# Keeping the split, transposed input of layer 0 in DRAM between two projections, and taking the gate projection two heads at a time

## The chip, the core and the metric

The kernel runs on one core of a Trainium2 chip. The metric is the device time of one execution in microseconds (us); the time before is the median of three runs. Compute engines of the core: TensorE (PE, matmuls; its weight loads are shown as PEld), VectorE (DVE), ScalarE (ACT) and GpSimd (POOL). SyncE (SP) issues all of this kernel's DMAs from one queue that works in order: a DMA that has to wait holds the ones behind it.

## The reference, cut to what matters

Two layers over x of 2048 rows by 1024. The first is sparse latent attention, the second a gated delta rule; each ends with a gated per-layer embedding. The change lies in the input projection of the first layer:

```
h = rms_norm(x, norm_w[0])
proj = h @ w_in
c_q, c_kv, k_idx, w_idx, z = jnp.split(proj, [256, 512, 640, 648], axis=-1)
c_q = rms_norm(c_q, g_cq); c_kv = rms_norm(c_kv, g_kv); k_idx = rms_norm(k_idx)
score = einsum("bqhs,bqh->bqs", relu(einsum("bqhd,bsd->bqhs", q_idx, k_idx)), w_idx)
_, sel = lax.top_k(score, 256)            # causal, per query
... attention over the selected latents gives o ...
return (o * jax.nn.silu(z)) @ w_out       # z has 8 heads of 128
```

So the same normalised h is needed by the latents (c_q, c_kv, k_idx, w_idx) and by the gates z.

## The kernel before, in words

A product of two float32 matrices is made of three matmuls: each operand is split into a high part (ACT copies it to the matmul's type) and a low part (the rest; DVE subtracts when the source is in PSUM, POOL when it is in SBUF). `split`, `split_sb` and `mm3_step` (lines 71 to 92) do this.

Phase 1 (up to about 865 us of the profiled execution) has two scopes. In `latents` the rows go in four super blocks (sb) of 512. `enter(sb, 3)` loads four blocks of 128 rows of x (`load_x`), normalises them, transposes each on PE against `ident` (8 transposes of 128x128, L209, tile `xT`), and splits the result from PSUM into `hT` (L78 on ACT, L79 on DVE). `latents(sb)` then multiplies hT with the weights of c_q, k_idx, c_kv and w_idx, while `enter` of the next super block is woven between. The normalised x is also stored to DRAM (`xn_d`, L189).

In `scores` four kinds of streams are woven on all engines: `index` (matmuls `il`, ACT relu `rl`, DVE adds into `score`), `topk` (13 rounds of counting above a threshold, half of the blocks on DVE, L729, half on ACT, L727, with some small POOL instructions that set the next threshold; then a selection on DVE that ends in `pen`, which SP stores and ACT sums, `penj`, L805), and the stream `rest`: `gates_z` for the four super blocks, then `proj_k` and `proj_v1`, then `proj_q`. `PLAN`, `WORK` and the weights of the parts give every piece of a stream a place on one scale, `weave` takes the pieces in the order of these places, and a scheduler then sets the order on each engine. At run time each engine works in that order.

`gates_z(sb)` needs hT again. Before the change it loads the normalised x back from `xn_d` (L179), transposes it again (32 transposes a super block, woven as `enter(sb, 2)`) and splits it again into four tiles of tag `c8`; then, head by head, it takes two weight tiles (`win`: a load `wr`, a split on ACT, L86, and POOL, L87, into a tile `w` of 4 buffers; the raw tiles `raw` have 3) and makes 24 matmuls of 512 columns (`pz`). ACT applies SiLU to the head (L370) and SP stores it (L371). After the fourth super block `proj_k` loads four tiles of the latents c_kv into the same four `c8` buffers.

## Time and profile before

| | before |
|---|---|
| median of 3 runs | 3472.86 us (3471.24 to 3486.31) |
| profiled execution | 3468.28 us, span 3466.6 us, mean granted clock 0.981 |
| PE busy | 3321.1 us (96% of the span) |
| DVE, ACT, POOL busy | 2102.7, 1882.7, 943.2 us |
| mean DMA rate | 90 GB/s |

PE is busy nearly all the time, and it works in order, so time is won where PE has less to do or waits less. The profiled execution is 4.6 us under the median of the runs. The profile counts overlapping matmuls once; a single matmul's duration is longer than the distance to the next.

### The profile page before, as it was taken

How to read it: one execution, taken by the hardware profiler on the slowest of the kernel's cores; microseconds unless marked ns; L12 is line 12 of the kernel's file. 1: busy time of each engine (PE TensorE's matmuls, PEld its weight loads, DVE VectorE, ACT ScalarE, POOL GpSimd, SP SyncE). 2: the span in 40 equal slices, each digit the busy share in tenths (PEclk: the TensorE clock that was granted, in tenths of full speed). 3: DMA queues.
4: the chain of work that ended last, by engine and by line, in shares of the span. 5: the costliest groups of instructions: out<-in, count | busy, mean ns of one | idle time of the engine just before them, and what ended most of it. 6: DMA issues, size and time to landing. Idle time of an engine off the chain costs nothing.

```text
span 3466.6 us, 52296 instructions
## 1 busy us (share of the span) xinstructions
PE 3321.1 (96%) x19082; PEld 2786.5 (80%) x19082; DVE 2102.7 (61%) x4566; ACT 1882.7 (54%) x3319; POOL 943.2 (27%) x1620
## 2 busy tenths in 40 slices
PE   8999988988899999999999999999999999899999
PEld 6778777877799999888887788887788888778887
DVE  5367896865588888622225667667667676633222
ACT  5366947675677777543335565555555555433221
POOL 2022435145645444211100221222121222321100
PEclk9999998999899999999999999999999999899999
DMA  6322344442522222422223222213222222233211
GB/s 218 114 77 68 102 148 145 172 152 98 183 78 85 80 85 74 136 95 64 72 64 94 58 50 55 53 45 93 54 58 50 58 51 57 86 130 116 73 34 72
DMA packets 325294, 311.71 MB, mean 90 GB/s; under 512 B 69448, under 2 KB 272808, under 8 KB 322984
## 3 DMA queue, kind: packets, MB, share of 16 engines
q1 hardware_dynamic: 325032, 308.33, 29.8%
q8 instruction: 150, 2.46, 0.3%
q14 instruction: 112, 0.92, 0.1%
HBM read 212.85 MB, written 95.42 MB: 89 GB/s over the span
## 4 chain that ended last, share of the span: by engine, by line
PE 53%; DVE 11%; DMA 4%; ACT 2%; POOL 2%; issue 2%; SPq 0%; DVEq 0%; ACTq 0%; POOLq 0%
PE pgm L91 3%; PE pgm L92 3%; PE pgm L90 3%; PE pt L1024 3%; DVE tmp L1639 3%; PE pom L91 2%; PE pom L90 2%; PE pom L92 2%; PE po L1044 2%; PE po L1045 2%; PE pBv L1521 2%; PE pBv L1522 2%; DVE inv L1642 2%; PE lg L92 2%; PE pBv L1523 2%
## 5 line engine op out<-in xcount | busy, mean ns | idle before, releaser
L79 DVE TENSOR_TENSOR pl<-pt,ph 128x512 fp32r<-128x512 f32 (+1 forms) x288 | 187.5, 657 | 45.8 <-ACT ph L78 43.6
L78 ACT ACTIVATE ph<-pt 128x512 fp32r<-128x512 f32 (+1 forms) x288 | 160.1, 564 | 97.5 <-PE pt L1024 90.3
L1006 ACT ACTIVATE pr<-pr,nm,qscale 128x1024 f32<-128x1024 f32 (+2 forms) x192 | 189.6, 988 | 41.0 <-DVE nm L1003 39.7
L423 DVE SCALAR_TENSOR_TENSOR score<-rl,wi,score 128x1024 f32<-128x1024 f32 (+7 forms) x154 | 169.0, 1119 | 39.6 <-ACT rl L415 38.8
L1247 DVE TENSOR_TENSOR gm<-ppm,gm 128x512 f32<-128x512 f32 x64 | 43.4, 689 | 244.4 <-ACT gm L1246 244.4
L1024 PE MATMUL pt<-ident,pr 128*128 128x128 f32 x1088 | 169.6, 276 | 7.6 <-ACT pr L1006 4.9
L729 DVE TENSOR_SCALAR_CACHE_REDUCE tkj<-score,t 128x1664 bf16<-128x1664 f32 (+3 forms) x91 | 121.7, 1353 | 86.8 <-POOL t L769 79.2
L415 ACT ACTIVATE rl<-il 128x1024 f32<-128x1024 f32 (+7 forms) x176 | 143.2, 819 | 54.8 <-PE il L92 49.2
L90 PE MATMUL pom<-wo,ym 128*128 128x512 f32 x432 | 171.0, 396 | 1.9 <-DVE y L1056 1.1
L91 PE MATMUL pom<-wo,ym 128*128 128x512 f32 x432 | 168.9, 391 | 1.3 <-POOL wo L87 1.3
L91 PE MATMUL pgm<-wm,xh 128*128 128x512 f32 x432 | 168.7, 390 | 1.5 <-DVE wm L82 1.5
L90 PE MATMUL pgm<-wm,xh 128*128 128x512 f32 x432 | 168.8, 391 | 0.6 <-ACT gm L1246 0.6
L92 PE MATMUL pom<-wo,ym 128*128 128x512 f32 x432 | 168.8, 391 | 0.0
L92 PE MATMUL pgm<-wm,xl 128*128 128x512 f32 x432 | 168.7, 390 | 0.0
L1044 PE MATMUL po<-pl,kv 128*128 128x256 f32 x576 | 162.8, 283 | 1.2 <-DVE pl L79 1.2
L1043 PE MATMUL po<-ph,kv 128*128 128x256 f32 x576 | 160.9, 279 | 1.5 <-ACT ph L78 1.5
L1045 PE MATMUL po<-ph,kv 128*128 128x256 f32 x576 | 162.1, 281 | 0.0
L87 POOL TENSOR_TENSOR ym<-yr,ym 128x1024 fp32r<-128x1024 f32 x32 | 77.1, 2409 | 303.5 <-ACT ym L86 303.4
L1246 ACT ACTIVATE gm<-pgm,rm_r 128x512 f32<-128x512 f32 x64 | 42.9, 684 | 183.8 <-PE pgm L91 117.5
L87 POOL TENSOR_TENSOR w<-wr,w 128x512 fp32r<-128x512 f32 x74 | 107.0, 1456 | 130.8 <-ACT w L86 122.8
L1752 ACT ACTIVATE qs<-pks,eg 128x128 f32<-128x128 f32 x120 | 44.0, 367 | 177.5 <-DVE y L1749 171.1
L727 ACT ACTIVATE tkj<-score,t 128x1920 bf16<-128x1920 f32 (+3 forms) x91 | 127.8, 1405 | 23.0 <-POOL t L769 19.8
(636 smaller groups left out, 10908.5 us busy)
## 6 DMA issues: line engine op xcount, KB each, us to landing
wBr<-in_b_w_in_dram SPq DMA_DIRECT2D x64, 512.0 KB
wr<-in_a_w_in_dram SPq DMA_DIRECT2D x74, 256.0 KB
yr<-yT_d SPq DMA_DIRECT2D x32, 512.0 KB
x<-in_x_dram SPq DMA_DIRECT2D x16, 512.0 KB
xn_d<-x SPq DMA_DIRECT2D x16, 512.0 KB
x<-xn_d SPq DMA_DIRECT2D x16, 512.0 KB
zT_d<-z SPq DMA_DIRECT2D x32, 256.0 KB
k_d<-k SPq DMA_DIRECT2D x16, 512.0 KB
```

The costliest lines, as they stand in the source:

```text
L78: nc.scalar.activation(hi, src, AF.Copy)
L79: nc.vector.tensor_tensor(lo, src, f32(hi), ALU.subtract)
L87: nc.gpsimd.tensor_tensor(lo, src, f32(hi), ALU.subtract)
L90: nc.tensor.matmul(dst, ah, bh, start=first, stop=False)
L91: nc.tensor.matmul(dst, ah, bl, start=False, stop=False)
L92: nc.tensor.matmul(dst, al, bh, start=False, stop=last)
L423: nc.vector.scalar_tensor_tensor(sc[:, s0:s1], rl[:, :s1 - s0], w, sc[:, s0:s1], ALU.mult, ALU.add)
L1006: nc.scalar.activation(pr[:, s0:s1], pr[:, s0:s1], AF.Exp, bias=nm, scale=sc, accum_out=den[:, i % 2, x:x + 1])
L1024: nc.tensor.transpose(pt[:, x * P:(x + 1) * P], probs[h, i][:, j * P:(j + 1) * P], ident)
L1043: nc.tensor.matmul(d, V[0][:, j], ph[:, c], start=st, stop=False)
L1044: nc.tensor.matmul(d, V[0][:, j], pl[:, c], start=False, stop=False)
L1045: nc.tensor.matmul(d, V[1][:, j], ph[:, c], start=False, stop=sp)
```

## The change

`enter` is now used in the `latents` scope alone. Its split hT is stored, in halves of the matmul operands as they are, to a DRAM tensor `hT_d`: `keep(sb, j)` stores two of the eight row groups (512 KB each) at four places within `latents(sb)`. `xn_d`, with its 16 stores and 16 loads of 512 KB, is gone. `gates_z(sb)` starts with four loads of 1 MB from `hT_d` into the four `c8` tiles (named `hz`), with no transpose and no split. It goes through the heads in pairs: for each half of the contraction (kh) two heads' weight tiles are used in turn, so two of the four `w` tiles are in use and the two for the next half are asked for ahead. Some numbers of the order change too. The diff, cut (numbers written as 7.0 for 7, and the like, are left out):

```diff
-    xn_d = dram.tile([S, D], F32, name="xn_d")
+    hT_d = dram.tile([NSB, P, KD, 2, SB], F32, name="hT_d")
...
-        rows = slice(n * P, (n + 1) * P)
-        if n in st1:
-            nc.sync.dma_start(xt, xn_d[rows, :])
-            return xt
-        nc.sync.dma_start(xt, a["x"][rows, :])
+        nc.sync.dma_start(xt, a["x"][n * P:(n + 1) * P, :])
...
-        nc.sync.dma_start(xn_d[rows, :], xt)
         return xt
...
-                yield i / 8 + b / 4
+                yield (i / 8 + b / 4) * 0.989 + 0.0
...
+    def keep(sb, j):
+
+        for k in (2 * j, 2 * j + 1):
+            nc.sync.dma_start(hT_d[sb, :, k], f32(st1["hT", sb][k]))
...
         def at():
-            return next(pos) / 22.0
+            n = next(pos)
+            if n in (6, 9, 12, 15):
+                keep(sb, (6, 9, 12, 15).index(n))
+            return n / 23.7367
...
     def gates_z(sb):
 
-        for f in enter(sb, 2):
-            yield f * 0.08
-        hT = st1.pop(("hT", sb))
-        ws = {}
+        hT = []
+        for j in range(0, KD, 2):
+            t = T("c8", 4, [P, 2, 2, SB], f"hz{sb}_{j}", F32R)
+            nc.sync.dma_start(f32(t), hT_d[sb, :, j:j + 2])
+            hT += [t[:, 0], t[:, 1]]
+
+        ws, order = {}, [(c, kh, x) for c in range(0, H, 2) for kh in range(2) for x in range(2)]
 
         def ahead(n):
-            if n < 16 and n not in ws:
-                ws[n] = win(5 + n // 2, n % 2, "w", 3 if st1["early"] else 4)
-
-        for c in range(H):
...
+            if n < len(order) and n not in ws:
+                c, kh, x = order[n]
+                ws[n] = win(5 + c + x, kh, "w", 4)
+
+        n = 0
+        for c in range(0, H, 2):
+            pz = [ps("pp", 4, f"pz{sb}_{c + x}") for x in range(2)]
+            for kh in range(2):
+                for x in range(4):
+                    ahead(n + x)
+                w = [ws.pop(n), ws.pop(n + 1)]
+                n += 2
+                for k in range(4):
+                    yield (c + kh + k / 4) / H
+                    for x in range(2):
+                        mm3_step(pz[x], w[x][:, 0, k], w[x][:, 1, k], hT[kh * 4 + k][:, 0], hT[kh * 4 + k][:, 1],
+                                 kh == 0 and k == 0, kh == 1 and k == 3)
+            for x in range(2):
+                z = T("o", 2, [P, SB], f"z{sb}_{c + x}")
+                nc.scalar.activation(z, pz[x], AF.Silu)
+                nc.sync.dma_start(zT_d[c + x, :, sb * SB:(sb + 1) * SB], z)
...
-        per = sum(sb * 4 + b + 1 for b in blocks) * 0.16 + 1.3
+        per = sum(sb * 4 + b + 1 for b in blocks) * 0.1741 + 1.1338
...
-                    parts = [([gates_z(sb) for sb in range(NSB)], 44), ([proj_q()], WQ),
+                    parts = [([gates_z(sb) for sb in range(NSB)], 42.1489), ([proj_q()], WQ),
...
-    WORK = {3: 100, 2: 72, 1: 46, 0: 14}
+    WORK = {3: 100, 2: 72, 1: 46, 0: 8}
...
-    PLAN = ({3: (0, 120), 2: (120, 260), 1: (300, 400), 0: (430, 470)},
-            {3: (122, 300), 2: (302, 415), 1: (417, 480), 0: (482, 530)}, 520)
+    PLAN = ({3: (0, 120), 2: (120, 256), 1: (300, 400), 0: (430, 470)}, {3: (122, 300), 2: (302, 415), 1: (417, 481), 0: (482, 530)}, 518)
```

Three places of the order follow. The first is PE's own order where `gates_z` of super block 2 ends and that of 3 begins; before the change:

```order
L92 MATMUL pz2_7_4493<-hT171_3934,w211_4496 128x512
L209 MATMUL xT3_0_0_4539<-ident_63,x212_4530 128x128 x4
L209 MATMUL xT3_0_1_4548<-ident_63,x212_4530 128x128 x4
L209 MATMUL xT3_1_0_4559<-ident_63,x217_4537 128x128 x4
L209 MATMUL xT3_1_1_4568<-ident_63,x217_4537 128x128 x4
L209 MATMUL xT3_2_0_4579<-ident_63,x218_4557 128x128 x4
L209 MATMUL xT3_2_1_4588<-ident_63,x218_4557 128x128 x4
L209 MATMUL xT3_3_0_4597<-ident_63,x219_4577 128x128 x4
L209 MATMUL xT3_3_1_4611<-ident_63,x219_4577 128x128 x4
L90 MATMUL pz3_0_4620<-hT213_4533,w221_4623 128x512
```

and after it (`hz3_0` is the first of the four loaded tiles, `w189` and `w191` the first weights of heads 0 and 1):

```order
L92 MATMUL pz2_7_4239<-hz2_6_3820,w187_4247 128x512
L90 MATMUL pz3_0_4326<-hz3_0_4318,w189_4330 128x512
L91 MATMUL pz3_0_4326<-hz3_0_4318,w189_4330 128x512
L92 MATMUL pz3_0_4326<-hz3_0_4318,w189_4330 128x512
L90 MATMUL pz3_1_4327<-hz3_0_4318,w191_4335 128x512
```

The 32 transposes are gone, and the first matmul of a super block follows the last one of the super block before. The second place is SP's queue at the same seam; before (`x212` to `x219` are the four blocks of normalised x, `wr` the raw weights, `pen15` the last result of the first top-k group):

```order
L179 DMA x212_4530<-xn_d_141 128x1024
L179 DMA x217_4537<-xn_d_141 128x1024
L371 DMA zT_d_100<-z2_5_4447 128x512
L179 DMA x218_4557<-xn_d_141 128x1024
L802 DMA pen_d_99<-pen15_4670 128x2048
L371 DMA zT_d_100<-z2_6_4490 128x512
L371 DMA zT_d_100<-z2_7_4527 128x512
L179 DMA x219_4577<-xn_d_141 128x1024
L220 DMA wr220_4621<-in_a_w_in_dram 128x4x128
```

and after:

```order
L213 DMA wr190_4333<-in_a_w_in_dram 128x4x128
L213 DMA wr192_4338<-in_a_w_in_dram 128x4x128
L345 DMA hz3_0_4318<-hT_d_141 128x2048
L345 DMA hz3_2_4320<-hT_d_141 128x2048
L345 DMA hz3_4_4322<-hT_d_141 128x2048
L371 DMA zT_d_100<-z2_6_4312 128x512
L371 DMA zT_d_100<-z2_7_4315 128x512
L345 DMA hz3_6_4324<-hT_d_141 128x2048
L213 DMA wr194_4343<-in_a_w_in_dram 128x4x128
L213 DMA wr196_4378<-in_a_w_in_dram 128x4x128
L213 DMA wr198_4383<-in_a_w_in_dram 128x4x128
L802 DMA pen_d_99<-pen15_4407 128x2048
```

Three of the four loads now stand ahead of the last z stores, and none behind the store of `pen15`; the fourth and the weight load `wr194` stand behind the stores of z2_6 and z2_7. The third place is ACT's order after the change, from the last `penj` of the first top-k group (`tkj2` are the first counts of the next group, `w193` and `w195` the weights of the second half of the first pair of heads):

```order
L805 ACTIVATE penj15_4441,got3_3940<-pen15_4407 128x2048
L370 ACTIVATE z2_6_4312<-pz2_6_4238 128x512
L86 ACTIVATE w193_4340<-wr192_4338 128x512
L370 ACTIVATE z2_7_4315<-pz2_7_4239 128x512
L727 ACTIVATE tkj2_2_218_4694,cnt2_4548<-score10_1628,t2_4554 128x1408
L727 ACTIVATE tkj2_3_223_4720,cnt2_4548<-score11_1629,t2_4554 128x1536
L86 ACTIVATE w195_4345<-wr194_4343 128x512
L86 ACTIVATE w197_4380<-wr196_4378 128x512
```

Before the change fourteen of the sixteen splits of transposed x (`hT`, L78) and the first weight split of the super block stand between `z2_7` and these counts.

## Rows read from the trace of the kernel before

**Rows 1.** The page's list of engines: busy time, share of the span, instructions.

```profile
PE 3321.1 (96%) x19082; PEld 2786.5 (80%) x19082; DVE 2102.7 (61%) x4566; ACT 1882.7 (54%) x3319; POOL 943.2 (27%) x1620
```

**Rows 2.** Busy time by stage: stretch, its length, then busy us (instructions) of PE, PEld, DVE, ACT, POOL, the mean granted clock, the DMA share and GB/s. The first, second, fourth and sixth are the seams where `gates_z` of super blocks 0, 1, 2 and 3 begin.

```profile
190.00:211.00 21.00, 19.99 (x107) 16.42 (x106) 15.24 (x33) 16.28 (x34) 7.15 (x37) 1.00 0.51 151
...
351.00:366.00 15.00, 11.46 (x66) 8.81 (x65) 12.19 (x25) 11.84 (x27) 3.89 (x9) 1.00 0.42 124
366.00:442.00 76.00, 75.13 (x336) 61.13 (x335) 67.61 (x72) 67.92 (x95) 36.78 (x78) 1.00 0.32 94
442.00:460.00 18.00, 13.91 (x72) 11.60 (x71) 16.46 (x34) 11.62 (x28) 2.69 (x11) 0.91 0.49 153
460.00:514.00 54.00, 51.79 (x228) 42.02 (x228) 53.69 (x55) 24.64 (x39) 25.82 (x15) 1.00 0.53 155
514.00:533.00 19.00, 10.63 (x44) 7.91 (x43) 15.15 (x42) 10.50 (x25) 4.14 (x11) 0.65 0.42 117
...
597.00:692.00 95.00, 92.74 (x463) 78.58 (x464) 81.59 (x117) 63.02 (x102) 17.99 (x43) 0.98 0.54 192
692.00:737.00 45.00, 36.66 (x236) 32.79 (x236) 22.30 (x51) 37.53 (x74) 17.41 (x76) 0.92 0.58 193
737.00:865.00 128.00, 117.61 (x621) 97.84 (x619) 82.94 (x172) 69.32 (x141) 65.33 (x134) 0.94 0.29 103
865.00:3466.00 2601.00, 2522.76 (x15190) 2135.01 (x15190) 1508.68 (x3664) 1346.78 (x2409) 658.24 (x1014) 0.98 0.27 77
```

**Rows 3.** What PE waited for between 192 and 600 us: us in total, times, longest.

```profile
PE xT L209 <- issue: 7.1, 1, 7.1
PE pk L90 <- DMA ckv<-ckv_d: 4.5, 1, 4.5
PE xT L209 <- DVE hT L79: 4.5, 3, 3.6
...
PE pz L92 <- POOL w L87: 1.7, 2, 1.4
```

**Rows 4.** The transposes of x, both uses (256 instructions; shortest, median and longest ns, first and last start), and the splits of the second use between 192 and 600 us (count, busy us, mean ns, idle before).

```profile
L209 PE MATMUL xT<-ident,x x256: 270/273/476, 7.6 to 527.2; 128*128 128x128 f32 x128
```

```profile
L79 DVE TENSOR_TENSOR hT<-xT,hT 128x256 fp32r<-128x256 f32 x64 | 23.7, 415 | 4.4 <-ACT hT L78 4.4
L78 ACT ACTIVATE hT<-xT 128x256 fp32r<-128x256 f32 x64 | 21.6, 399 | 13.9 <-DVE hT L79 11.5 <-PE xT L209 2.2
```

**Rows 5.** PE in order of time (start, duration): one group of four transposes and the matmul that follows it.

```profile
199.46 0.63 PE L209 MATMUL xT<-ident,x 128*128 128x128 f32 x4
199.85 0.50 PE L90 MATMUL il<-kidx_h,qi 128*128 128x512 f32 x1
```

**Rows 6.** PE in order of time at the fourth seam; the number in brackets is the idle time before.

```profile
514.31 1.91 PE L209 MATMUL xT<-ident,x 128*128 128x128 f32 x16
523.31 1.09 PE L209 MATMUL xT<-ident,x 128*128 128x128 f32 x4 [7.09 <-issue]
528.59 0.79 PE L90 MATMUL pz<-hT,w 128*128 128x512 f32 x1 [1.00 <-ACT w L86]
...
533.62 0.39 PE L92 MATMUL pz<-hT,w 128*128 128x512 f32 x1
533.85 0.39 PE L90 MATMUL pz<-hT,w 128*128 128x512 f32 x1
```

**Rows 7.** DVE and ACT at the fourth seam: the last `pen` of the first top-k group on DVE, its `penj` on ACT, and the first count of the next group on DVE.

```profile
511.03 0.69 DVE L801 TENSOR_SCALAR pen<-pen 128x2048 bf16<-128x2048 bf16 x1
521.45 1.41 DVE L729 TENSOR_SCALAR_CACHE_REDUCE tkj<-score,t 128x1152 bf16<-128x1152 f32 x1 [0.30 <-POOL t L756]
```

```profile
511.81 1.91 ACT L805 ACTIVATE penj<-pen 128x2048 bf16<-128x2048 bf16 x1 [4.34 <-DVE pen L801]
```

**Rows 8.** A load of 1 MB into a `c8` tile after the last super block: its issue on SP, and PE's first matmul that reads it.

```profile
591.71 0.42 SPq L527 DMA_DIRECT2D ckv<-ckv_d  x1
```

```profile
597.08 0.80 PE L90 MATMUL pk<-ckv,wk 128*128 128x512 f32 x1 [4.51 <-DMA ckv<-ckv_d]
```

**Rows 9.** The start of the program: SP's fourth load of x (it stands behind the first store of normalised x, L189), and PE's fourth group of transposes and first product.

```profile
7.87 0.43 SPq L181 DMA_DIRECT2D x<-in_x_dram  x1
```

```profile
17.10 1.94 PE L209 MATMUL xT<-ident,x 128*128 128x128 f32 x8 [1.90 <-DVE x L188]
20.39 0.79 PE L90 MATMUL ncq<-hT,w 128*128 128x512 f32 x1 [1.35 <-ACT w L86]
```

**Rows 10.** Groups of ACT and of POOL between 520 and 600 us: the counts of the second top-k group, and the weight splits.

```profile
L727 ACT ACTIVATE tkj<-score,t 128x1536 bf16<-128x1536 f32 x11 | 17.2, 1566 | 0.0
L727 ACT ACTIVATE tkj<-score,t 128x1408 bf16<-128x1408 f32 x11 | 16.1, 1465 | 9.2 <-POOL t L769 9.2
L86 ACT ACTIVATE w<-wr 128x512 fp32r<-128x512 f32 x16 | 9.9, 625 | 1.7 <-POOL thr L761 1.7
```

```profile
L87 POOL TENSOR_TENSOR w<-wr,w 128x512 fp32r<-128x512 f32 x16 | 20.6, 1295 | 12.3 <-ACT w L86 12.3
```

**Rows 11.** The first seam: the last two stores of the `latents` scope on SP, and the first instruction of the `scores` scope that waits for them on ACT.

```profile
190.88 1.77 SPq L293 DMA_DIRECT2D ckv_d<-nkv3o  x2
```

```profile
195.86 1.02 ACT L415 ACTIVATE rl<-il 128x1024 f32<-128x1024 f32 x1 [0.27 <-DMA ckv_d<-nkv3o]
```

**Rows 12.** PE's wait for ACT in the stage of `proj_v1`.

```profile
720.34 0.79 PE L90 MATMUL qi<-cq,wiq 128*128 128x512 f32 x1 [5.19 <-ACT va L561]
```

More of the change, by code (lines that the diff above doesn't have):

```diff
@@ L171, in load_x @@
         n = sb * 4 + b
-        if n == 3 and n not in st1:
+        if n == 3:
             xt = T("lat", 2, [P, D], f"x{next(uid)}")
@@ L188, in load_x, with enter @@
         nc.vector.scalar_tensor_tensor(xt, xt, r, st1["gain"], ALU.mult, ALU.mult)
-        nc.sync.dma_start(xn_d[rows, :], xt)
         return xt
-    def enter(sb, xbufs):
-        xs = [load_x(sb, b) for b in range(xbufs - 1)]
+    def enter(sb):
+        xs = [load_x(sb, b) for b in range(2)]
         hT = None
@@ L197, in enter @@
             for i in range(2):
-                yield i / 8 + b / 4
+                yield (i / 8 + b / 4) * 0.989 + 0.0
                 if hT is None:
-                    n = KD if st1["early"] else 2
-                    hT = [T(*(("hT", 2) if st1["early"] else ("c8", 4)), [P, n, 2, SB], f"hT{next(uid)}", F32R)
-                          for _ in range(0, KD, n)]
-                    st1["hT", sb] = [hT[k // n][:, k % n] for k in range(KD)]
-                if i == 0 and b + xbufs - 1 < 4:
-                    xs.append(load_x(sb, b + xbufs - 1))
+                    hT = T("hT", 2, [P, KD, 2, SB], f"hT{next(uid)}", F32R)
+                    st1["hT", sb] = [hT[:, k] for k in range(KD)]
+                if i == 0 and b + 2 < 4:
+                    xs.append(load_x(sb, b + 2))
                 pt = ps("pp", 4, f"xT{sb}_{b}_{i}")
@@ L209, in enter @@
                     nc.tensor.transpose(pt[:, k * P:(k + 1) * P], xs[b][:, (i * 4 + k) * P:(i * 4 + k + 1) * P], ident)
-                ts_ = slice(b * P, (b + 1) * P)
-                m = min(n, 4)
-                for k in range(i * 4, i * 4 + 4, m):
-                    h = hT[k // n][:, k % n:k % n + m]
-                    split(pt[:, (k - i * 4) * P:(k - i * 4 + m) * P].rearrange("p (k n) -> p k n", k=m),
-                          h[:, :, 0, ts_], h[:, :, 1, ts_])
+                h = hT[:, i * 4:i * 4 + 4]
+                split(pt.rearrange("p (k n) -> p k n", k=4), h[:, :, 0, b * P:(b + 1) * P], h[:, :, 1, b * P:(b + 1) * P])
+    def keep(sb, j):
+        for k in (2 * j, 2 * j + 1):
+            nc.sync.dma_start(hT_d[sb, :, k], f32(st1["hT", sb][k]))
     def win(c, kh, tag, bufs):
@@ L396, in index @@
         query(0)
-        at = 1.3
+        at = 1.1338
         for h in range(H):
@@ L598, in phase1 @@
                 st1["widx"] = T("widx", 1, [P, KD, 16], "widx_w", F32R)
-                for _ in enter(0, 3):
+                for _ in enter(0):
                     pass
@@ L608, in phase1 @@
                         near_bias()
-                    weave(latents(sb, kidx, wi_all), *([enter(sb + 1, 3)] if sb + 1 < NSB else []))
+                    weave(latents(sb, kidx, wi_all), *([enter(sb + 1)] if sb + 1 < NSB else []))
                     st1.pop(("hT", sb), None)
@@ L909, in tile_trunk @@
     PRL, PRS, AHEAD = 4, 4, 2
-    C0, DELTA = 1.5, 7
+    C0, DELTA = 1.5, 7.0
     def near_bias():
@@ L1079, in phase2 @@
         pens = T("pens", 1, [P, P * NB * (NB + 1) // 2], "pens", BF16)
-        cost = [4 * g + 3 + C0 for _, g in order]
+        cost = [4.0 * g + 3 + C0 for _, g in order]
         begin = list(itertools.accumulate([0] + cost))
@@ L1510, in project @@
                                 yield at
-                        if i == GI and sb == 1 and k == 2:
+                        if i == GI and (sb, k) == (1, 2):
                             gb = m["gb"] = T("raw", 3, [P, NC, P], f"gb{j}", where=pre)
@@ L1515, in project @@
                         if n + 1 < 64 and n % 32 != 31:
-                            if sb == 0 and k == 0:
+                            if (sb, k) == (0, 0):
                                 made["raw"] = load_weights(n + 1)
-                            elif sb == 1 and k == 0:
+                            if (sb, k) == (1, 0):
                                 ready[n + 1] = raw_weights(n + 1, made.pop("raw"))
@@ L1535, in ch, with by4 @@
             return slice(c * P, (c + 1) * P)
-        def by4(name, mm, sink, at):
+        def by4(name, mm, sink, at, more=0.0):
             for g in range(2):
-                yield at
+                yield at + g * more
                 pp = ps("g", 3, f"{name}_{g}")
@@ L1819, in ahead @@
                         if k % 2:
-                            yield at + (c * 4 + k // 2 + 1) / 9 * (0.25 if part == 0 else 1 / n)
+                            yield at + (c * 4 + k // 2 + 1) / 9 * (0.25 if part == 0 else 1.0 / n)
                     nc.vector.tensor_tensor(xt[:, cs], pp, xt[:, cs], ALU.add)
```

33 lines of the change are left out of this document (9 added, 24 removed).

## The prediction

> **What bounds the kernel now.** I read first the list of engines, where PE is busy 96% of the span [rows 1]; then busy time by stage, with the stretches cut where `gates_z` begins a super block (a "seam") [rows 2]; then PE's waits between 192 and 600 us [rows 3] and PE in order of time at the seams [rows 5, 6]; last what the other engines do there [rows 7, 10, 11]. PE works in order, so phase 1 ends when PE's list ends, and everything from 865 us on stands in the same order in both kernels; I take its 2601 us as unchanged [rows 2]. The reader should see in rows 2 that PE is not full at the seams: it is busy 11.46 of 15 us, 13.91 of 18 and 10.63 of 19, and in the last two the mean granted clock is 0.91 and 0.65, which is a mixture of the full level of 2.4 GHz with the lower one of 1.2. Between the seams PE is full, but DVE nearly is too: 67.61 of 76 us, then 53.69 of 54. So in 366 to 514 us two engines bind, and a gain on PE counts in full only if DVE is relieved as well. It is: 64 of its splits go [rows 4].
>
> **What goes.** (1) 128 transposes. A group of four takes 0.39 us until the next matmul starts [rows 5], so 32 groups cost 12.5 us at full clock. A single transposition lasts 273 ns [rows 4], but they overlap. The Trainium skill (TensorE: Matmul & The Clock Gate, Part 4: PE-mode transpose) prices one at about 275 ns in a kernel; the trace agrees on the duration, but by that price the 128 would be worth 35.2 us and the forecast some 23 us lower. The spacing decides against it.
>
> (2) Idle PE at the seams. From rows 2: 15 − 11.46 = 3.5 us, 18 − 13.91 = 4.1, 19 − 10.63 = 8.4, and 1.0 at the first: 17.0 in all. The longest is 7.1 us before a transposition [rows 3, 6]. The chain behind it: the last top-k result of the first group ends on DVE at 511.7 us, the next group's preparation follows, and only then do DVE's splits of transposed x get their turn, at about the time of the next counts, 521.45 [rows 7]; PE has no buffer left until then.
>
> (3) Lost clock at the seams. In 442 to 460 us a mean clock of 0.91 means 3.2 us at half speed; in 514 to 533, 0.65 means 13 us. With PE's idle time taken out, I put the busy part at half speed at 3 and 8.5 us, of which half is lost: 5.7 us.
>
> (4) PE's 4.5 us for the first latents of `proj_k` [rows 3, 8]. That load may start when the last reader of its `c8` tile has ended. Before, that is after a quarter of the last head's 24 matmuls, 18 from the end; now it is after a quarter of the last pair's 48, 36 from the end. At 0.23 us a matmul [rows 6] the load can start 4.1 us sooner: nearly all of the wait goes, and 1.2 us at half clock behind it. 5.5 us.
>
> (5) The start. The fourth load of x stands on SP behind a store of normalised x that waits for DVE, until 7.87 us; the weights come behind more such stores, and PE waits 1.90 and 1.35 us for them [rows 9]. The stores go, and the four loads are issued together. 3 us.
>
> Together 12.5 + 17.0 + 5.7 + 5.5 + 3.0 = 44 us.
>
> **What comes.** (6) Stores: 32 of 512 KB instead of 16, within `latents`; they wait for no engine, since hT is complete by then. (7) Loads: 16 of 1 MB instead of 16 of 512 KB. DMA is 32% to 53% busy in the stretches from 190 to 533 us [rows 2], so bytes alone cost nothing there. A 1 MB load takes 4.9 us from the end of its issue (592.1) to its first reader (597.08) [rows 8]. At a seam the first three loads may start 36, 24 and 12 matmuls before the old super block ends, so 8.2, 5.4 and 2.7 us ahead, and each is needed 8.2 us after that at the earliest: hidden, with index matmuls between even more so. I take 1 us for the second and third seams. If that cover fails (SP held by something else), up to 4.9 us each.
>
> (8) The first seam: the loads reuse memory of the `latents` scope and stand behind its last stores, whose issue ends at 192.65; ACT's first instruction of the new scope starts at 195.86 [rows 11]. 192.7 + 4.9 = 197.6 us; the index matmuls ahead of the first `pz` need that relu and the next, so PE arrives at about the same time or a little sooner. 2 us (bounds 0 and 4.9).
>
> (9) The fourth seam. ACT's new order puts `w193` behind the last `penj`, and `w195` behind the first two counts of the next group. These start about when DVE's does, 521.45, so 9.7 us after the last `pen` ends at 511.7 [rows 7]; two counts of 1.47 and 1.57 us, ACT's split of 0.63 and POOL's of 1.30 [rows 10] give 15 us from that `pen` to a usable `w195`. PE needs it 27 matmuls (6.1 us) after it starts the super block. DVE's `pen` should come about 15 us sooner than now: 5 of PE's early gain, and 10 to 12 of the 17.8 us of splits that stood before it (three quarters of 23.7 [rows 4]). PE comes sooner by about as much, so it meets the wait, some 7 us, and I add 2 for the clock behind it: 9 us. So a stall stays here; what is late is no longer a split of x but a weight.
>
> (10) Weights in pairs. Two `w` tiles come free together and have 24 matmuls, 5.4 us, to be filled (the second 6.1, since its head comes three matmuls later): ACT 0.63, then POOL twice 1.30, 3.2 us. Below, 0. Above, ACT is at the start of its two counts when the tiles come free, and these wait for their threshold (9.2 us in 11 rounds, 0.8 each): 0.8 + 3.0 + 0.63 + 2.6 = 7.0 us [rows 10], 0.9 too late, in each of the 14 halves that run without index matmuls: 13 us. I take 3, near the lower end, because PE waited only 1.7 and 1.0 us for weights before [rows 3, 6].
>
> What comes: 1 + 2 + 9 + 3 = 15, so PE should reach `proj_k` 29 us sooner.
>
> **What of it arrives.** From 597 us the rest of phase 1 runs beside the later top-k groups. In 597 to 692 us DVE is busy 81.59 of 95, and in 692 to 737 PE only 36.66 of 45 [rows 2], with a wait of 5.19 for ACT, which is held by counts [rows 12]. Where these groups set the pace, only their own shift counts, about 15 us. I take 22, in the middle between 15 and 29. The profiled execution's 3468.3 becomes 3446.3; the median of the runs lies 4.6 higher, so **3451 us**. Half a per cent, 17.4 us, is about what a measurement of this kernel tells from no change.
>
> **Rivals.** A, *the top-k groups hold the end* (0.18): PE arrives early and waits for relu and counts in 597 to 737; only about 12 us remain: 3461. For it: DVE's 53.69 of 54 and rows 12. Against: DVE and ACT lose 23.7 and 21.6 us of work [rows 4].
>
> B, *the tiles come late* (0.10): SP holds the loads or the weights behind a `pen` or z store that waits for DVE or ACT, so each seam keeps a stall. The stalls and the lost clock of terms 2 and 3 then stay, and the gain is 12.5 + 5.5 + 3 less 9, so 12: 3461. The Trainium skill (DMA: Bandwidth & Descriptors, Bandwidth) speaks for it: it gives 6.15 us for 1 MB, and by that four loads in a row would take longer than the 10.9 us in which PE uses them; its price would put the time near 3456. The load in rows 8 was faster, with another 1 MB load close behind it.
>
> C, *more* (0.10): the fourth seam and the pairs cost little and all arrives: 44 − 7 = 37, 3436.
>
> D, *slower* (0.06): the pairs starve. The place is the `w` tiles: in every half PE waits for ACT and POOL, because ACT is within counts or relu whenever a pair comes free. The halves number 32; without term 10 PE gains 32. At 1 us a half the gain is gone, and at 1.6 us a half the kernel is 19 us slower: 3492. Against it: term 10 finds 0.9 at most, and in 18 of the halves index matmuls stretch the 5.4 us.
>
> **Numbers.** The likeliest, 22 us, has 0.56 with its own range 3444 to 3458, of which 0.04 lies within the half per cent. Faster: 0.52 + C 0.10 = 0.62. Same: 0.04 + A 0.18 + B 0.10 = 0.32. Slower: D, 0.06. The range takes in C below (3434, where the first seam costs nothing too) and A and B above, with term 10 at its upper bound beside A's loss: 3461 + 10 = 3471, so 3470. 3434 to 3470 leaves out D and little else.
>
> **What would show it.** No `xT` beside `pz`; the first `pk`, now at 597 us, 25 to 30 us sooner and its wait gone; at the fourth seam a PE wait for ACT or POOL `w` of 5 to 9 us in the first pair, instead of 7.1 before a transposition; the last `pen` of the first group some 15 us sooner; the end of phase 1 (865) some 22 us sooner, and the rest as long as before. It is wrong if PE's waits for `w` sum to more than 20 us, if PE waits for `hz` loads at every seam, or if the 597 us mark moves 25 us and the 865 mark less than 15.

## The result and the profile after

The changed kernel takes 3443.38 us (median of 7 runs, 3436.22 to 3455.19); the kernel before, 3485.02 (median of 7, 3471.24 to 3487.19). The ratio on record, taken over the runs, is 0.9901, with a 95% interval of 0.9882 to 0.9920: faster by 1.0% (the two medians alone would give 0.9881). The forecast was 3451 within 3434 to 3470. The two profiled executions are 3468.28 and 3443.02 us, 25.3 us apart; the medians are 41.6 apart, and "The offset" below says what is known of the rest.

Engines after, which answers to [rows 1]:

```profile
PE 3304.1 (96%) x18954; PEld 2773.9 (81%) x18954; DVE 2090.1 (61%) x4502; ACT 1862.2 (54%) x3255; POOL 950.1 (28%) x1620
```

PE is 17.0 us less busy, with 128 instructions fewer. Next busy time by stage of the kernel after, with the columns of [rows 2]. The cuts are the first index matmul, the first `pz` matmul of each super block, the last `pz`, the first `pva` and `pgq`, and the end of phase 1. PE's idle time is the length less PE's busy time.

```profile
190.26:201.11 10.85, 5.09 (x17) 3.61 (x18) 4.02 (x6) 4.04 (x7) 6.00 (x36) 0.71 0.70 244
201.11:355.38 154.27, 154.27 (x689) 125.24 (x689) 113.27 (x134) 99.27 (x131) 34.08 (x44) 0.99 0.31 96
...
441.49:504.31 62.82, 57.70 (x251) 47.24 (x249) 62.12 (x70) 32.08 (x50) 25.08 (x25) 0.97 0.54 171
504.31:573.91 69.60, 61.60 (x260) 49.24 (x259) 46.29 (x76) 52.03 (x77) 41.23 (x98) 0.95 0.58 182
...
839.80:3441.28 2601.48, 2523.62 (x15190) 2137.27 (x15190) 1511.84 (x3664) 1346.67 (x2409) 658.90 (x1014) 0.98 0.27 77
```

Behind phase 1 both executions take 2601.5 us. So the whole 25.3 us of the profiles is in phase 1, which ends at 839.8 instead of 865.1. From the first index matmul to the first `pk`, in one row, before and then after:

```profile
190.66:597.08 406.42, 380.13 (x1731) 308.33 (x1731) 324.25 (x432) 288.07 (x442) 153.06 (x303) 0.98 0.35 104
```

```profile
190.26:576.15 385.89, 366.34 (x1608) 296.99 (x1609) 306.60 (x364) 266.40 (x372) 154.92 (x295) 0.97 0.44 138
```

This stretch is 20.5 us shorter. PE's busy time fell by 13.8 us and its idle time from 26.3 to 19.6; 4.5 us of that is the wait for the first load of `proj_k` [rows 8], so without it the idle time fell only from 21.8 to 19.6. The stalls of the four seams were to go, and they are almost as long as before, in other places. What PE waited for, 190 to 600 us, after (total, times, longest), to be read beside [rows 3]:

```profile
PE il L90 <- ACT rl L415: 7.0, 3, 5.8
PE pz L90 <- DMA hz<-hT_d: 4.6, 1, 4.6
PE pz L90 <- DVE qi L79: 4.2, 1, 4.2
PE pz L92 <- POOL w L87: 1.5, 1, 1.5
...
```

The 5.8 us stand at the first seam. ACT and PE there:

```profile
196.02 1.67 ACT L86 ACTIVATE w<-wr 128x512 fp32r<-128x512 f32 x3 [4.89 <-DMA ckv_d<-nkv3o]
197.59 1.59 ACT L415 ACTIVATE rl<-il 128x1024 f32<-128x1024 f32 x2
```

```profile
198.65 0.80 PE L90 MATMUL il<-kidx_h,qi 128*128 128x512 f32 x1 [5.76 <-ACT rl L415]
```

ACT waits for the last store of the latents, as before [rows 11], and then makes three weight splits before the first relu. PE has filled its index buffers by 192.9 us and stops. Before, it had other work at this place: six matmuls of `qi` and then eight of the transposes, with 1.0 us of idle time, until the relu let it go on at 196.93. The first row of the `qi`, and the second group of transposes:

```profile
193.35 0.44 PE L90 MATMUL qi<-cq,wiq 128*128 128x512 f32 x1
...
196.36 0.66 PE L209 MATMUL xT<-ident,x 128*128 128x128 f32 x4 [0.97 <-DVE flags L617]
```

The transposes are gone, and the order that follows from the change has these `qi` matmuls behind the first `pz`. The row of the first seam also shows a granted clock of 0.71. Now the fourth seam: DVE's last `pen` of the first group, ACT, SP and PE.

```profile
502.93 0.69 DVE L801 TENSOR_SCALAR pen<-pen 128x2048 bf16<-128x2048 bf16 x1
```

```profile
503.71 1.91 ACT L805 ACTIVATE penj<-pen 128x2048 bf16<-128x2048 bf16 x1 [3.51 <-DVE pen L801]
...
505.62 0.58 ACT L370 ACTIVATE z<-pz 128x512 f32<-128x512 f32 x1
...
515.98 1.47 ACT L727 ACTIVATE tkj<-score,t 128x1408 bf16<-128x1408 f32 x1 [8.77 <-DVE tkj L729]
...
519.01 1.65 ACT L86 ACTIVATE w<-wr 128x512 fp32r<-128x512 f32 x3
```

```profile
506.23 1.33 SPq L371 DMA_DIRECT2D zT_d<-z  x2
507.65 0.39 SPq L345 DMA_DIRECT2D hz<-hT_d  x1
```

```profile
515.91 0.80 PE L90 MATMUL pz<-hz,w 128*128 128x512 f32 x1 [4.64 <-DMA hz<-hT_d]
...
519.67 0.51 PE L90 MATMUL pz<-hz,w 128*128 128x512 f32 x1 [0.83 <-ACT w L86]
```

These rows are one chain. ACT waits for `pen` before its last `penj`; the SiLUs of z2_6 and z2_7 stand behind that `penj`; their stores stand ahead of the fourth load of hT on SP; the load is issued at 507.65 and PE's first reader starts at 515.91. Behind that, `w195` stands behind two counts that could not start before 515.98. With 1.5 us more for POOL's half of `w195` PE loses 6.9 us.

### The profile page after: what moved, and what is told of

Read it like the earlier page. It is cut to its first block, busy times and chain, and to the rows that moved or that the text cites. A ratio compares the mean times of both kernels' runs of the same rounds, so it can differ in the third digit from the quotient of the medians.

```text
span 3441.3 us, 51940 instructions
## 1 busy us (share of the span) xinstructions
PE 3304.1 (96%) x18954; PEld 2773.9 (81%) x18954; DVE 2090.1 (61%) x4502; ACT 1862.2 (54%) x3255; POOL 950.1 (28%) x1620
## 4 chain that ended last, share of the span: by engine, by line
PE 54%; DVE 11%; DMA 4%; POOL 2%; ACT 2%; issue 2%; SPq 0%; DVEq 0%; ACTq 0%; POOLq 0%
PE pgm L91 3%; PE pgm L92 3%; PE pgm L90 3%; PE pt L1024 3%; DVE tmp L1639 2%; PE pom L90 2%; PE pom L92 2%; PE pom L91 2%; PE pBv L1521 2%; PE po L1044 2%; PE pBv L1522 2%; PE po L1045 2%; PE lg L92 2%; PE pBv L1523 2%; PE lg L90 2%
## 5 line engine op out<-in xcount | busy, mean ns | idle before, releaser
L78 ACT ACTIVATE ph<-pt 128x512 fp32r<-128x512 f32 (+1 forms) x288 | 159.8, 564 | 97.7 <-PE pt L1024 89.0
L90 PE MATMUL lg<-kv,q 128*128 128x512 f32 (+2 forms) x320 | 139.7, 437 | 0.7 <-DVE mx L997 0.7
```

The costliest lines, as they stand in the source:

```text
L78: nc.scalar.activation(hi, src, AF.Copy)
L90: nc.tensor.matmul(dst, ah, bh, start=first, stop=False)
```

## Experiments

Two theories of the 25 us stood at the start. *Terms*: the sum of the prediction is right term by term, so transposes, relief of DVE and ACT, and shorter stalls make the gain, and the new numbers and the pairs make none. *Elsewhere*: the new numbers of the order, or the pairs, make much of it. The first four kernels tell these apart, the next four the stalls that remain. "From the first index matmul" leaves the latents out, which differ between executions (below).

**The old numbers.** The edit:

```diff
-        per = sum(sb * 4 + b + 1 for b in blocks) * 0.1741 + 1.1338
+        per = sum(sb * 4 + b + 1 for b in blocks) * 0.16 + 1.3
...
-    WORK = {3: 100, 2: 72, 1: 46, 0: 8}
+    WORK = {3: 100, 2: 72, 1: 46, 0: 14}
...
```

> The changed kernel with the numbers of the order as they were before (0.16 and 1.3 for index, 44 for the gates, 22.0 and 1.0 in the latents, WORK 14 for the last super block, PLAN 260, 480, 520). Theory S (the gain is in the structure: transposes gone, seams 2 and 3 without a stall): the profiled execution stays within 6 us of the changed kernel's 3443.0, and the end of phase 1 within 6 us of 839.8. Theory N (a good part comes from the new numbers): 10 us or more of the 25 go back, 3453 or higher. In the latents S expects PE to start its first product at 17.5 as in the changed kernel; if the 2.6 us that PE waits for the squares of c_q at 37 us come from the numbers, that wait falls to about 0.2 and the first index matmul comes 2 to 3 us before 190.3.

Measured: 3452.03 us (3445.26 to 3454.01), ratio to before 0.9915 (0.9892 to 0.9937); profile 3452.5. To the first `pk`, and from there to the end of phase 1, with the old numbers; then the second stretch alone in the changed kernel and in the kernel before (their first stretches stand above):

```profile
189.06:577.92 388.86, 368.50 (x1608) 296.82 (x1609) 310.42 (x362) 262.67 (x368) 155.83 (x294) 0.97 0.43 136
577.92:850.40 272.48, 249.25 (x1317) 210.32 (x1315) 193.10 (x344) 174.56 (x323) 104.55 (x261) 0.95 0.41 142
```

```profile
576.15:839.80 263.65, 243.83 (x1317) 206.60 (x1315) 185.43 (x342) 171.89 (x319) 103.83 (x259) 0.97 0.42 146
```

```profile
597.08:865.10 268.02, 247.02 (x1316) 209.21 (x1316) 186.85 (x338) 169.80 (x314) 100.73 (x251) 0.95 0.43 149
```

Neither theory holds as it stands: the profile is 9.5 us longer and phase 1 ends 10.6 later, where S allowed 6 and N wanted 10 in the whole time. In these profiles up to `pk` the old numbers cost 3.0 us, behind it 8.8 (272.5 against 263.7). With them the stretch behind `pk` is 4.5 us longer than before the change; with the new ones it is 4.4 shorter. How much of the 8.8 belongs to the numbers is not shown: the mean clock differs too (0.95 and 0.97), two profiles of the kernel before differ by 3.4 us there (below), and the ratios of the runs, 0.9915 and 0.9901, have intervals that overlap. In the latents PE's wait for the squares at 37 us fell from 2.6 to 0.9, and the first index matmul came 1.2 us sooner, which is within what other executions show.

**One head at a time.** The loop of the kernel before, on the loaded hT:

```diff
-        for c in range(0, H, 2):
-            pz = [ps("pp", 4, f"pz{sb}_{c + x}") for x in range(2)]
+        for c in range(H):
...
+            ck = chunk(hT, get, f"pz{sb}_{c}")
...
```

> The changed kernel with the gate heads taken one at a time, as before the change; the loads of the stored hT stay. Theory P0 (the pairs are neutral, because outside the seams PE hardly waited for weights in either kernel: 1.7 us before, 2.3 after): within 5 us of the changed kernel, 3438 to 3448, the stall at the fourth seam stays at 5 to 9 us. Theory P+ (the pairs give the weights of a half more time and so save PE waits): 8 us or more slower, with PE waits for w from ACT and POOL of 8 us or more in sum. Theory P- (pairs starve PE, as the prediction's term of 3 us has it): 3 us faster.

Measured: 3442.48 us (3434.16 to 3455.26), 0.9900 (0.9873 to 0.9927). The runs can't tell it from the changed kernel, as P0 has it. In the profile, though, it is 4.3 us longer from the first index matmul to the first `pk` (390.2 against 385.9), and 2.8 longer to the end of phase 1: the fourth seam waits 6.8 us for a load of hT and 3.0 for weights, above the 5 to 9 of P0, and PE waits 11.6 us for relus where it was 7.0. In this execution latents that were 4.7 us shorter cover it. So the pairs show no cost, and may gain a little.

**The transposes alone.**

```diff
             pz = [ps("pp", 4, f"pz{sb}_{c + x}") for x in range(2)]
+            for x in range(2):
+                for k in range(4):
+                    nc.tensor.transpose(pz[x][:, k * P:(k + 1) * P], f32(hT[0][:, 0, k * P:(k + 1) * P]), ident)
```

> The changed kernel with 128 extra transposes of 128x128 on PE, eight at the start of each pair of heads, written into the pair's own PSUM tiles and overwritten by its products; nothing else is added (no split, no load). They stand where PE is full. Theory spacing: 32 groups of four at 0.39 us, 12.5 us; with the stalls at the first and fourth seams taking in a little, 11 to 13 us later at the end of phase 1 (851 to 853), and 3453 to 3457 for the execution. Theory duration: 128 times 0.273 us, 35 us later, 3478. Theory cover (PE's list is not what ends phase 1): under 4 us.

Measured: 3461.62 us (3455.54 to 3473.54), 0.9951 (0.9931 to 0.9970). Its stretches to and from the first `pk`:

```profile
186.01:585.17 399.16, 380.20 (x1737) 309.84 (x1737) 315.55 (x374) 272.76 (x382) 155.91 (x310) 0.98 0.42 133
585.17:853.19 268.02, 247.38 (x1317) 210.56 (x1315) 180.07 (x332) 165.76 (x310) 98.98 (x245) 0.95 0.42 144
```

To `pk` it takes 13.3 us more than the changed kernel (399.16 against 385.89): the spacing prices a transpose (12.5), not its duration (35). The end of phase 1 is at 853.2, at the upper edge of the expectation, but only because the latents were 4.3 us shorter here; counted from the first index matmul it comes 17.6 later, 4.4 of that behind `pk`. The execution and the runs lost 18 to 19 us; 5.5 us of the execution's lie behind phase 1, where nothing was changed.

**The splits alone, on ACT and DVE.**

```diff
                 z = T("o", 2, [P, SB], f"z{sb}_{c + x}")
+                for k in range((3, 3, 2, 0)[c // 2]):
+                    split(f32(hT[k + 4 * x][:, 0, :256]), z[:, :256], z[:, 256:])
```

> The changed kernel with 64 extra copies on ACT and 64 extra subtractions on DVE, 128x256 each as the splits of transposed x were, sixteen in each super block of the gates within its first three pairs; they are made from the loaded hT into the tile that SiLU overwrites afterwards, and PE has nothing added. Theory relief (DVE is near full in 366 to 504 us, so its work sets when the first top-k group ends): the last pen of the first group, at 503.6 in the changed kernel, comes 6 us or more later, and the end of phase 1 4 to 10 us later. Theory slack (the counts leave gaps on DVE that take the work in): the pen moves under 3 us and the end of phase 1 under 3 us.

Measured: 3464.06 us (3456.30 to 3468.12), 0.9955 (0.9937 to 0.9974). The last `pen` ends at 521.5 instead of 503.6, and phase 1 takes 672.0 us from the first index matmul instead of 649.5: 22.5 more, beyond what the relief theory expected. But ACT waited 22.4 us in its copies and 6.8 in SiLU for DVE, which this edit brought in by sharing a tile. So it was repeated on DVE alone:

```diff
+                    if k % 2 == 0:
+                        s = T("spare", 1, [P, 224], f"spare{sb}_{c}_{kh}_{k}", BF16)
+                        nc.vector.tensor_tensor(s, f32(hT[kh * 4 + k][:, 0, :224]), f32(hT[kh * 4 + k][:, 1, :224]), ALU.subtract)
```

> The changed kernel with 64 extra subtractions on DVE alone, 128x224 each, sixteen in each super block of the gates, written to a tile that nobody reads; ACT and PE have nothing added. This repeats the run with the extra splits without its side effect, that ACT's copies and SiLU waited for DVE (22.4 and 6.8 us in that run). Some 48 of them, 19 us, stand ahead of the last pen of the first group. Theory relief: that pen comes 12 to 19 us later than 503.6 (counted from the first index matmul), and the end of phase 1 8 to 15 us later. Theory coupling (the 22 us of the earlier run came from ACT's waits for DVE, not from DVE's load): the pen 10 to 19 us later all the same, but the end of phase 1 under 5 us.

Measured: 3454.37 us (3449.42 to 3464.96), 0.9941 (0.9920 to 0.9962). Its added operations on DVE (186 to 600 us), its last `pen`, and PE's wait at the fourth seam:

```profile
L367 DVE TENSOR_TENSOR spare<-hz 128x224 bf16<-128x224 f32 x64 | 32.6, 510 | 1.9 <-DMA hz<-hT_d 1.1
```

```profile
513.94 0.69 DVE L804 TENSOR_SCALAR pen<-pen 128x2048 bf16<-128x2048 bf16 x1
```

```profile
522.38 0.80 PE L90 MATMUL pz<-hz,w 128*128 128x512 f32 x1 [7.88 <-ACT w L86]
```

Counted from the first index matmul, `pen` comes 14.7 us later, the first `pk` 13.2 later (399.1 against 385.9) and the end of phase 1 9.2 later (658.7 against 649.5). The operations took 32.6 us, more than the 23.7 of the splits that the change removed [rows 4]; in that proportion the relief is worth some 10 us at `pk` and 7 at the end of phase 1 (an estimate). It reaches PE through the counts, where PE waits 7.9 us for `w195`, and through the relus, for which it waits 12.1 us where it was 7.0.

**The fourth seam, three ways.** All z stores from ACT's queue; only the stores of z2_6 and z2_7 from POOL's; only the fourth load of hT of super block 3 from POOL's:

```diff
-                nc.sync.dma_start(zT_d[c + x, ...], z)
+                nc.scalar.dma_start(zT_d[c + x, ...], z)
```

```diff
+                (nc.gpsimd if (sb, c) == (2, 6) else nc.sync).dma_start(zT_d[c + x, ...], z)
```

```diff
+            (nc.gpsimd if (sb, j) == (3, 6) else nc.sync).dma_start(f32(t), hT_d[sb, :, j:j + 2])
```

> The changed kernel with the 32 stores of z issued by ACT instead of SP. At the fourth seam nothing then stands ahead of the fourth load of hT on SP but the loads before it, and the order puts the weights w193, w195, w197 and w199 ahead of the first count on ACT. In the changed kernel PE waits there 4.6 us for the load, then 0.8 and 1.5 us for w195. Theory both (load and weight hold the seam, one behind the other): at most 3 of these 6.9 us stay, and with the half clock behind them the end of phase 1, counted from the first index matmul (649.5 us in the changed kernel), shrinks by 6 to 10 us. Theory next wait (the first counts, held back behind four weights, delay the second top-k group by as much, and 32 issues of 0.3 to 0.4 us on ACT cost what the stall gave): under 3 us either way.

> The changed kernel with only two stores moved: those of z2_6 and z2_7, issued by POOL instead of SP. On SP the fourth load of hT then follows the third directly; on ACT one count (1.47 us) instead of two stands ahead of w195. Theory load (the late load alone makes the stall): the 4.6 us wait goes and the seam keeps under 3 us, 5 to 8 us less from the first index matmul to the end of phase 1. Theory weight (w195 is set by the first counts, at about 516 us, whether the load is late or not): PE comes 4 us sooner to w195 and waits there 5 to 8 us instead; the stall as a whole shrinks by 2 us at most.

> The changed kernel with one load moved: the fourth load of hT of super block 3 is issued by POOL instead of SP. It no longer stands behind the stores of z2_6 and z2_7, and the order puts w195 and w197 ahead of both first counts on ACT. Theory load: like the run that moves the two stores, 5 to 8 us less. Theory weight: only here, where both causes go, does the stall fall from 6.9 us to 3 or less, with 6 to 10 us less to the end of phase 1, while the run that moves the two stores gains 2 us at most.

Measured, in this order: 3443.62 us (0.9908, 0.9889 to 0.9928), 3437.62 (0.9892, 0.9872 to 0.9912), 3440.13 (0.9895, 0.9875 to 0.9915). From the first index matmul to the end of phase 1: 645.9, 644.2 and 645.1 against 649.5. But the first of these is no gain. In the changed kernel, as in the other runs, the engines wait ahead of this mark for a branch (L671), and with the z stores on ACT the wait falls behind it; DVE in the changed kernel, then in this run:

```profile
836.86 0.69 DVE L509 TENSOR_TENSOR qg<-pgq,qf 128x512 f32<-128x512 f32 x1 [4.34 <-DVEq L671]
```

```profile
839.49 0.95 DVE L517 RECIPROCAL qscale<-qinv 128x128 f32<-128x128 f32 x1 [4.34 <-DVEq L671]
```

PE's first product behind phase 1 starts 651.4 us after the first index matmul in this run, and 650.9 in the changed kernel: theory *next wait* holds for it, as the time of its runs says too. PE's two waits at the seam, with the two stores moved:

```profile
510.02 0.50 PE L90 MATMUL pz<-hz,w 128*128 128x512 f32 x1 [0.72 <-DMA hz<-hT_d]
516.44 0.61 PE L90 MATMUL pz<-hz,w 128*128 128x512 f32 x1 [4.76 <-ACT w L86]
```

and with the load moved, with ACT's split of `w195` and the loads' time from issue to landing (count, KB, median us):

```profile
512.54 0.50 PE L90 MATMUL pz<-hz,w 128*128 128x512 f32 x1 [3.66 <-DMA hz<-hT_d]
514.13 0.79 PE L90 MATMUL pz<-hz,w 128*128 128x512 f32 x1 [1.08 <-ACT w L86]
```

```profile
513.45 0.63 ACT L86 ACTIVATE w<-wr 128x512 fp32r<-128x512 f32 x1 [8.63 <-DMA wr<-in_a_w_in_dram]
```

```profile
hz<-hT_d SPq DMA_DIRECT2D x15, 1024.0 KB, 6.8
hz<-hT_d POOLq DMA_DIRECT2D x1, 1024.0 KB, 8.7
```

The stall is 5.5 us in the one and 4.7 in the other, from 6.9; theory *load* wanted under 3 in both, and theory *weight* 3 or less in the second. With the load in time in the first, PE comes sooner to `w195` and waits there, as theory *weight* said of the first; with the weight ahead of the counts, the load itself took 8.7 us from POOL's queue and the raw weight came late too. With all z stores on ACT PE still waits 4.8 us for a split that waits for its raw weight. The load, the raw weight and the first count come within 2.3 us of each other there (512.5, 513.4 and 514.8 in the third run), so taking away one shows the next. The stall fell by 1.4 and 2.2 us where the totals fell by 5.4 and 4.4; the part that lies elsewhere cannot be put down to these edits.

**The first seam.** The relu tiles go to the memory of the enclosing scope, so they need not wait for the latents' last store:

```diff
-                    rl = T("rl", 3, [P, 1024], f"rl{sb}_{b}_{h}_{s0}")
+                    rl = T("rl", 3, [P, 1024], f"rl{sb}_{b}_{h}_{s0}", where=keys)
```

> The changed kernel with the three relu tiles in the memory of the enclosing scope, so that ACT needn't wait for the last store of the latents before the first relu; nothing else changes but the order that follows (three relus ahead of the first three weight splits). In the changed kernel PE idles 5.8 us at the first seam and then runs at half clock, 5.1 us lost from there to super block 1. Theory scope (the wait is for the memory that the latents' store still reads): the idle time falls to under 2 us and most of the clock loss goes, 6 to 10 us less from the first index matmul to the end of phase 1. Theory DVE (the next thing in line, the first score tiles, wait for the same store, so that the relu tiles fill up after three): 2 to 4 us less. Rival: under 1.5 us, because the first loads of hT and the weights, which also need that memory, set when PE can go on.

Measured: 3434.67 us (3427.45 to 3439.58), 0.9878 (0.9858 to 0.9898). The two stretches up to the second super block of the gates, and ACT's first relus:

```profile
189.15:200.23 11.08, 9.69 (x42) 7.42 (x43) 6.50 (x10) 7.72 (x11) 6.03 (x36) 1.00 0.69 242
200.23:347.23 147.00, 147.00 (x665) 119.37 (x665) 113.33 (x130) 95.65 (x127) 34.92 (x44) 1.00 0.32 100
```

```profile
191.30 1.62 ACT L415 ACTIVATE rl<-il 128x1024 f32<-128x1024 f32 x2 [1.29 <-PE il L92]
```

Theory *scope* holds: relu starts at 191.3, PE makes 42 matmuls before the first `pz` instead of 17, the clock stays at 1.00, and the two stretches take 158.1 us instead of 165.1. Of these 7.0 us 4.4 are idle time and 2.7 PE's busy time, which is the clock. At the end of phase 1 5.9 remain, just under the 6 to 10 of the theory. The same idle time and half clock stood in none of the rows before the change, so this is a cost of the change.

**Both.** The relu tiles and the two moved stores together:

> The changed kernel with both single edits that gained by themselves: the relu tiles in the enclosing scope (alone 5.9 us less from the first index matmul to the end of phase 1, 649.5 to 643.6) and the stores of z2_6 and z2_7 issued by POOL (alone 5.4 us less). Theory apart (two seams 300 us from each other, so the gains add): 10 to 12 us less, 638 to 640, and a median of 3428 to 3432. Theory same slack (what PE gains at the first seam is waited for again at the fourth, where the first counts of the second top-k group set w195): 6 to 8 us less, and a median of 3434 to 3437.

Measured: 3432.80 us (3423.91 to 3437.71), 0.9866 (0.9845 to 0.9888). From the first index matmul to the end of phase 1 640.8, 8.8 us less: between the two theories, and the median is 2 us from the relu tiles alone, which these runs can't tell apart. It beats the kernel before by 1.3%; that it beats the changed kernel, by some 0.3%, is likely and not shown, since the two intervals overlap a little (0.9845 to 0.9888 and 0.9882 to 0.9920).

**The kernel before once more.**

> The kernel before the change once more, for a second profile of it. If the latents differ between executions of one kernel by as much as in the kernels above that share the changed latents (first index matmul at 185.5 to 190.3 us), this one's comes within 187 to 194 us; from the first index matmul to the end of phase 1 it should take 674.4 us as in the first profile, within 3 us. If instead the stretch behind the first index matmul varies by more than 5 us, differences of single profiles there are no evidence.

Measured: 3483.25 us, one execution. The second profile, and the first below it:

```profile
190.59:680.00 489.41, 462.22 (x2105) 375.82 (x2106) 396.07 (x527) 343.84 (x529) 167.04 (x333) 0.98 0.38 118
680.00:868.53 188.53, 167.50 (x944) 143.38 (x942) 115.88 (x243) 113.73 (x226) 86.70 (x221) 0.93 0.38 130
868.53:3481.51 2612.98, 2531.93 (x15190) 2141.80 (x15190) 1513.11 (x3664) 1346.59 (x2409) 658.11 (x1014) 0.98 0.27 76
```

```profile
190.66:680.00 489.34, 461.91 (x2104) 376.15 (x2105) 396.27 (x527) 343.86 (x529) 166.87 (x333) 0.98 0.38 118
680.00:865.10 185.10, 165.24 (x945) 141.39 (x943) 114.82 (x244) 114.01 (x226) 86.93 (x221) 0.94 0.39 133
```

Up to 680 us they agree within 0.1 us. Behind it the same work takes 3.4 us more, a little beyond the 3 us expected, and behind phase 1 2613.0 against 2601.5 [rows 2]. So, as far as two profiles show it, phase 1 up to `proj_v1` compares well from single profiles, and the rest does not.

## Why the prediction was right, and where its steps were not

The time lies inside the range and near the forecast: 3443.0 for the profiled execution where 3446.3 was forecast. The median comes in 7.6 us under 3451. That is partly good fortune; several terms were off and offset each other.

**Transposes (1)**: 12.5 forecast; 13.3 measured by adding them. Right for transposes that stand where PE is full. The duration that the Trainium skill gives (TensorE: Matmul & The Clock Gate, Part 4: PE-mode transpose), about 275 ns (measured there with bf16), was rightly left out of the sum: as a price, 35 us for the 128, it is refuted where they stand in fours and eights. Those that the change took out weighed a little more. Up to the first `pk` both kernels make the same 1608 other matmuls and the kernel before 122 of its transposes besides (six stand ahead of the stretch); PE's busy time fell by 13.8 us while the clock took some 2 us more (next paragraph), so the 122 took nearly 16.

**Stalls and clock of the seams (2, 3, and the costs 6 to 10)**: 22.7 less 15, so 7.7 us net, were forecast. Idle time fell by 2.2. For the clock, the mean of a stretch mixes 1.2 and 2.4 GHz, and (1 − mean) times its length is half of its time at half clock: by the rows after, 3.1 + 1.5 + 1.9 + 3.5 = 10.0 us from the first index matmul to the last `pz`; before, cut at the same events, 1.9 + 4.2 + 2.6 = 8.7, from these rows:

```profile
365.56:458.59 93.03, 88.39 (x404) 72.51 (x405) 83.10 (x105) 78.57 (x120) 38.51 (x88) 0.98 0.36 106
458.59:528.59 70.00, 59.10 (x265) 47.50 (x264) 68.65 (x92) 32.14 (x59) 28.22 (x24) 0.94 0.49 145
528.59:592.56 63.97, 62.73 (x270) 50.62 (x270) 33.51 (x53) 51.47 (x80) 40.78 (x92) 0.96 0.40 110
```

Where PE idles at half clock, only the idle time is lost, and that is counted already. Most of it lies in two places, after and then before:

```profile
194.86:198.65 3.79, 0.00 (x1) 0.00 (x1) 0.09 (x2) 2.63 (x5) 2.42 (x34) 0.50 0.52 138
```

```profile
519.55:528.59 9.04, 4.00 (x16) 3.01 (x17) 8.04 (x21) 4.92 (x15) 0.81 (x4) 0.50 0.15 39
```

Half of these 3.8 and 5.0 us comes off: the clock cost about 8.1 us after and 6.2 before, so 2 more, and the idle time fell by 2.2. Net nothing, where 7.7 us were forecast: this is the step that failed. Most of it is term (8), which measured 7. I forecast 2 us at the first seam, because ACT's first relu set PE's start before [rows 11] and the loads of hT would land soon after. The idle time there is 5.8 us (1.0 before), with half clock behind it. What I missed is that the work that PE had there was cover, not only cost: with the eight transposes gone, and the six `qi` matmuls moved by the order that follows, nothing lay between the index matmuls and the relu, and ACT's new order put three weight splits (1.7 us) ahead of it. It is not the new numbers that do this: with the old ones put back, the order there is the same and PE idles 5.6 us. The run with relu tiles elsewhere gives the size: 7.0 us.

**The fourth seam (9)**: 9 us forecast; 6.9 idle, and some 3 of lost clock in its super block. The size was right, the place half so: the first of the waits was for the fourth load of hT, 7.9 us from the end of its issue to its reader, where I had taken 4.9 from one load [rows 8]. Rival B was true at this one seam, and `w195`, which I had named, stands right behind. The figure of the Trainium skill (DMA: Bandwidth & Descriptors, Bandwidth), 6.15 us for 1 MB, measured there for loads that GpSimd issues, was nearer than my row: in the run with the fourth load moved, the median of the 15 other loads is 6.8 us from issue to landing. At the seams of super blocks 1 and 2 no load was waited for, as forecast; a wait of 4.2 us for DVE's `qi` at 446.6, with 1.9 of clock by the row of that stretch, was new and not foreseen: term (7) had 1 us.

**`proj_k` (4)**: the wait for its first load is gone, as forecast. The first `pk` came 20.9 us sooner, at 576.15, not 25 to 30.

**The start (5)**: PE starts its first product at 17.5 instead of 20.4, 2.9 us sooner, as forecast; in this execution only 0.4 was left at the first index matmul. Nine other kernels with the same code there had it at 185.5 to 191.3 us, on average 2.7 sooner than before, so the 3 was fair.

**Pairs (10)**: 3 us of cost forecast; one head at a time measures the same in the runs and is 4.3 us longer up to `pk` in the profile, so no cost shows. Rival D falls with it.

**DVE's relief**: that two engines bind was right; taking back somewhat more than the relief on DVE alone costs 13.2 us at the first `pk` and 9.2 at the end of phase 1. The last `pen` came 8 us sooner and not 15. Why only half is open.

**What arrives**: 29 at `proj_k` less 7 behind it gave 22. It was 20.9, and then 4.4 more. Rival A's pull fits what the old numbers give: with them the stretch behind `pk` grows by 4.5 us. But the new numbers, to which I gave no term at all, take 8.8 off it in these profiles, part of which may be the clock. A retuned table in a diff is an edit with a price of its own, and here, by these profiles, it made up for what was missing at the first seam.

**The offset**: I put the median 4.6 us above the profiled execution. For the changed kernel it is 0.4, and for the kernel before 16.7 above (3485.02 against 3468.28). So the median that I started from, 3472.86 of three runs, was low, and that the changed kernel's median came so near the forecast is luck. The first profile of before was one of its shorter executions behind phase 1: its two have 2601.5 and 2613.0 there, the changed kernel 2601.5, the ten kernels with the same code there 2599.8 to 2607.4 (2609.8 with the z stores on ACT, where the branch wait falls behind the mark). The runs go with the clock: over the 38 runs of the kernel before that stand beside the experiments, each 0.001 of mean granted clock more goes with 2.7 us less (a straight line through them). Their mean is 3477.1 us at 0.9789, that of the seven of the changed kernel 3445.2 at 0.9806; of these 31.9 us some 5 go with the clock, and the 27 left (an estimate) are near the 25.3 of the profiles. Why the clock is higher in the one set stays open.

## What to carry to other kernels

Work that is removed from a busy engine may have been the cover of a wait that is nowhere in the profile: before taking it out, look at what that engine waits for at this place without it, here the relu behind a scope's last store. Where a stall has been cleared once, read when the next two inputs come; at the fourth seam three came within 2.3 us, and each of three edits alone moved the stall to its neighbour. A mark that closes a stretch must have the same waits ahead of it in every kernel that is compared. And give the retuned numbers of an order their own line in the sum, with a run that puts them back.

## What the runs showed of the hardware

Two executions of one program, with the same order on PE, agree within 0.1 us over 489 us and then differ by 15, for the most part where the granted clock differs. The same 485 PE instructions in the second layer, first profile of before, then second:

```profile
1890.00:1982.28 92.28, 85.57 (x485) 69.26 (x484) 50.06 (x95) 50.80 (x88) 16.84 (x39) 0.98 0.31 69
```

```profile
1897.63:1997.12 99.49, 94.03 (x485) 75.33 (x484) 50.93 (x95) 50.87 (x88) 16.74 (x39) 0.88 0.28 64
```

At a mean clock of 0.88 instead of 0.98 they take 7.2 us more. So a difference of single profiles under some 10 us is evidence only in a stretch that repeats.
